# A few small numbers in one tile: every large tile starts 32 or 128 bytes earlier

## The chip, the core and the metric

The kernel runs on one core of a Trainium2 chip. The metric is the device time of one execution in microseconds. Three runs of the kernel before took 2431.29 to 2432.54 us, with a median of 2431.8 us.

Five engines work in parallel, each on its own list of instructions: PE (TensorE: weight loads and matmuls), DVE (VectorE), ACT (ScalarE), POOL (GpSimd, here mainly an issuer of DMAs) and SP (which issues DMAs). They wait for each other through semaphores. Tiles live in a memory of 128 partitions; an address below is the byte at which a tile starts within each partition.

## The reference

One layer of a streaming encoder on 256 tokens of 2048 features: a SwiGLU block, a gated mixer of two recurrent branches, a cross attention to 256 memory tokens, a second SwiGLU block, and a final norm. All of it is float32.

```python
x = x + 0.5 * swiglu(rms_norm(x, ffn1_norm[l]), ffn1_w_up[l], ffn1_w_down[l])
h = rms_norm(x, mix_norm[l])
proj = h @ w_in[l]                       # columns split into the branches' inputs and gates
y_a = ...                                # HGRN2 recurrence, normed, times silu(g_a)
y_b = ...                                # conv, RG-LRU scan, times gelu(gate_b)
merged = g[:, :, 0, :] * (y_a @ w_branch_a[l]) + g[:, :, 1, :] * (y_b @ w_branch_b[l])
x = x + merged @ w_out[l]
x = x + cross_attention(rms_norm(x, xattn_norm[l]), rms_norm(mem, mem_norm[l]), ...)
x = x + 0.5 * swiglu(rms_norm(x, ffn2_norm[l]), ffn2_w_up[l], ffn2_w_down[l])
return rms_norm(x, final_norm)
```

Each SwiGLU has 5632 hidden columns, so the two blocks hold most of the arithmetic.

## The kernel before

**How a product is made.** A float32 operand is split into a high and a low part of a shorter type (`split`: ACT copies the high part `h`, DVE subtracts it to get the low part `l`), and a product is a sum of matmuls high by high, high by low, and low by high. Weights arrive by DMA as `raw` tiles of 128 x 2048 floats (8192 bytes per partition) and are split into tiles `h` and `l` of the same size; in the SwiGLU blocks differences of weights (`td`, split into `h` and `tl`) save products. Activations stand in tiles of 128 x 1024 (4096 bytes) as `xh`, `xl`, `hidop`, `ops` and others. Each matmul has two operands in that memory: the stationary one, 128 columns wide, which a weight load (PEld) brings into the array, and the moving one, mostly 512 columns wide, which streams through.

- In the SwiGLU blocks (`three`), and in the products `rows_product`, a slice of an activation tile is stationary and a slice of `h`, `l` or `tl` moves: rows such as `acc<-h,xh` name the moving operand first, and then the stationary one.
- In `product` (middle part of the layer) the slice of the weight tile is stationary and the activation moves: `acc<-ops,h`.
- At the start the memory tokens, in tiles `ms` of 8192 bytes, are stationary, and their weights move: `acc<-h,ms` and `acc<-l,ms`.
- Hidden activations are transposed by PE against a constant identity: `acc<-vt,ev`.

**Where tiles lie.** Pools are laid out one behind the other, and each tile is rounded up to 32 bytes: `const` (small constants and the residual stream `x`), `big` (9 tiles of 8192 bytes), `slots` (24 tiles of 4096 bytes), `small` (a few bytes each), and then, in one region used in turn, the pools of a stage. In a SwiGLU stage this region holds four further tiles of 8192 bytes, pool `more`, which join the nine of `big` in one ring of 13: a tile `raw`, `h`, `l`, `td`, `tl`, `ev` or `ms` gets whichever of the 13 is free. In the middle stage the region holds other, smaller tiles, and the weight tiles use the nine of `big` alone.

**What sets the order.** Every instruction is recorded first (`Flow.record`), then a planner (`Flow.arrange`) orders each engine's list and chooses a place in the ring for each tile by estimated costs, and `Flow.emit` issues them all from one line. So the profile has line L478 for everything, and one goes by the names of tiles.

**What the change touches.** Three small tiles: `eps` (one number per partition, a bias for square roots), `rmtok` (two numbers: the norm factors of the memory tokens) and `ssm` (their sums of squares, in `head_squares`).

Of the kernel before, what the change touches and what calls it, by code (L numbers as in the profile page):

```python
# [9 lines left out]
F32 = mybir.dt.float32  # L10
F32R = mybir.dt.float32r
ACT = mybir.ActivationFunctionType
ALU = mybir.AluOpType

P = 128
T = 256
D = 2048
# [22 lines left out]
PAD = 16  # L40
# [149 lines left out]
class Flow:  # L190
# [22 lines left out]
    def pool(self, name, bufs, scope=None, **kw):  # L213
        self.pools.append(Pool(self, name, bufs, scope, **kw))
        return self.pools[-1]
# [267 lines left out]
def block_kernel(tc: tile.TileContext, xT, xin, memT, mem, vec, gfin, bgate, lruw, wu1, wd1, win, wv,  # L483
                 wg, wab, wout, wq, wk, wvm, wo, wu2, wd2, out_):
    flow = Flow(tc)
    pe, dve, act, sp, gps = flow.queues
    pool = flow.pool

    const = pool("const", 1)
    flow.share("big", pool("big", 9), 9)  # L490

    def big(name, dt=F32R):
        return flow.shared("big", [P, 2048], dt, name)

    slots = pool("slots", 24)
    small = pool("small", 2)
# [36 lines left out]
    warm = bank("warm")  # L533
    for _ in range(16):
        pe.matmul(warm[:, :P], ones, ones, start=True, stop=True)
    eps = const.tile([P, 1], F32, name="eps")
    act.activation(eps, ones[:, :1], ACT.Copy, scale=EPS)
    xt = [const.tile([P, 4 * T], F32, name=f"x{q}") for q in range(4)]
    x = [xt[k // 4][:, (k % 4) * T:(k % 4 + 1) * T] for k in range(KT)]
# [540 lines left out]
            self.tiles.append(self.cur[:, i * 512:(i + 1) * 512])  # L1080
            return self.tiles[-1]

    ms1, rmtok = BigOperands(), const.tile([P, 2], F32, name="rmtok")

    def head_memory(kq):
        m = slot(name="mem")
# [4 lines left out]
                ms1.add(m[:, j:j + T], col("mem_norm", 4 * kq + j // T))  # L1091

    def head_squares():
        ss = small.tile([P, 2 + PAD], F32, name="ssm", tag="ssm", bufs=1)[:, :2]
        for t in range(2):
            m = big("memory", F32)
            sp.dma_start(m, mem[t])
            act.activation(m, m, ACT.Square, accum_out=ss[:, t:t + 1])
        act.activation(ss, ss, ACT.Sqrt, bias=eps, scale=1.0 / D)
        dve.reciprocal(out=rmtok, in_=ss)  # L1100

    head.update({kq: lambda kq=kq: head_memory(kq) for kq in range(4)})
    todo = [[] for _ in range(11)]
    for p in range(8):
        todo[p].append(lambda p=p: head_x(p))
        if p % 2:
            todo[p].append(lambda p=p: sums1[p // 2]())
    todo[3].append(head_squares)
    for c in range(4):
        todo[6 + c].append(lambda c=c: head_residual(c))  # L1110
# [594 lines left out]
```

## Time and profile before

| | us |
|---|---|
| median of three runs | 2431.8 |
| the profiled execution | 2431.7 |
| its span, first to last instruction | 2429.9 |
| PE busy with matmuls | 2419.3 |
| PE busy with weight loads (beside the matmuls) | 2005.8 |
| DVE busy | 2090.5 |
| ACT busy | 1442.8 |

The first SwiGLU block fills the span up to about 760 us, the mixer and the attention stand between 760 and 1720 us, and the second SwiGLU block runs from about 1720 us to the end. Matmuls are pipelined: the duration shown for one is longer than the step from its start to the start of the next, so the pace of PE is read from starts. The timeline merges neighbours on one engine that have the same operands; a row gives the start of the first, the time to the end of the last, and their count. The step of one matmul is then the start of the next row minus the start of this one, divided by the count.

### The profile page before, as it was taken

The page shows a single profiled execution, that of the slowest core. Times are in us where ns is not written, and L with a number is a line of the kernel's source. Part 1 is how long each engine was busy: PE and PEld are TensorE (multiplying, and loading weights), DVE is VectorE, ACT ScalarE, POOL GpSimd, SP SyncE. Part 2 cuts the span into 40 slices and gives each one's busy share as a digit, 9 for nine tenths or more (in the row PEclk, how much of TensorE's full clock was granted, in tenths as well). Part 3 has the DMA queues.
Part 4 walks back from the last instruction along what each step waited for, and adds up shares of the span by engine and source line. Part 5 has one row for each costly group of instructions (what it writes and reads, how often), then busy time and mean ns, then how long its engine had stood idle before and what let it go on. Part 6 is the DMA issues. An engine that isn't in the chain of part 4 may idle for free. (4 is left out here: it accounts for less than half of the span.)

```text
span 2429.9 us, 31006 instructions
## 1 busy us (share of the span) xinstructions
PE 2419.3 (100%) x12105; PEld 2005.8 (83%) x12105; DVE 2090.5 (86%) x2270; ACT 1442.8 (59%) x1432; POOL 88.6 (4%) x149
## 2 busy tenths in 40 slices
PE   9999999999999999999999999999999999999998
PEld 8888788888888888888888888888878788888887
DVE  7899999999996677888787878887789999999994
ACT  8765666666665544445853455555676666665563
POOL 0000000000000000000000000000000000000000
PEclk9999999999999999999999999999999999999999
DMA  9675877777774578798898898887798667667773
GB/s 364 242 274 180 260 259 255 249 258 248 254 256 177 182 290 325 268 349 330 328 339 329 327 372 337 331 312 260 291 372 299 255 247 264 257 258 259 260 273 113
DMA packets 101235, 674.37 MB, mean 278 GB/s; under 512 B 11232, under 2 KB 12000, under 8 KB 27232
## 3 DMA queue, kind: packets, MB, share of 16 engines
q1 hardware_dynamic: 79776, 523.40, 57.5%
q0 software_dynamic: 20592, 147.86, 18.9%
q8 instruction: 95, 1.56, 0.2%
q10 hardware_dynamic: 720, 1.13, 0.1%
q14 instruction: 52, 0.43, 0.0%
HBM read 581.12 MB, written 62.91 MB: 265 GB/s over the span
## 5 line engine op out<-in xcount | busy, mean ns | idle before, releaser
L478 DVE TENSOR_TENSOR l<-raw,h 128x2048 fp32r<-128x2048 f32 (+2 forms) x425 | 860.1, 2028 | 173.9 <-ACT h L478 80.3
L478 ACT ACTIVATE h<-raw 128x2048 fp32r<-128x2048 f32 (+2 forms) x425 | 722.1, 1705 | 383.5 <-PE acc L478 176.2
L478 PE MATMUL acc<-h,xh 128*128 128x512 f32 x1237 | 476.8, 393 | 0.5 <-DVE ev L478 0.3
L478 PE MATMUL acc<-h,xl 128*128 128x512 f32 x1237 | 475.5, 392 | 0.0
L478 ACT ACTIVATE h<-td 128x1024 fp32r<-128x1024 f32 (+1 forms) x262 | 322.9, 1241 | 227.9 <-DVE td L478 171.7
L478 DVE TENSOR_TENSOR tl<-td,h 128x1024 fp32r<-128x1024 f32 (+1 forms) x262 | 375.6, 1448 | 8.6 <-PE acc L478 5.2
L478 PE MATMUL acc<-h,hidop 128*128 128x512 f32 x1408 | 360.7, 394 | 0.0
L478 PE MATMUL acc<-h,ops 128*128 128x512 f32 x1408 | 336.9, 391 | 0.0
L478 PEld LDWEIGHTS acc<-h,hidop 128*128 128x128 f32 x1408 | 262.9, 188 | 58.8
L478 PEld LDWEIGHTS acc<-h,ops 128*128 128x128 f32 x1408 | 262.7, 188 | 54.0
L478 PE MATMUL acc<-ops,h 128*128 128x512 f32 x1152 | 282.1, 393 | 0.2 <-DVE ops L478 0.2
L478 PEld LDWEIGHTS acc<-h,xh 128*128 128x128 f32 x1237 | 232.0, 188 | 54.9 <-ACT h L478 1.6
L478 PEld LDWEIGHTS acc<-h,xl 128*128 128x128 f32 x1237 | 232.4, 188 | 51.6
L478 PEld LDWEIGHTS acc<-ops,h 128*128 128x128 f32 x1152 | 211.4, 188 | 42.4 <-DVE ops L478 0.6
L478 PE MATMUL acc<-l,hidop 128*128 128x512 f32 x704 | 195.7, 392 | 0.0
L478 PE MATMUL acc<-tl,xh 128*128 128x512 f32 x636 | 177.4, 395 | 0.6 <-DVE tl L478 0.6
L478 PE MATMUL acc<-l,ops 128*128 128x512 f32 x704 | 174.3, 389 | 0.0
L478 PE MATMUL acc<-l,xh 128*128 128x512 f32 x601 | 169.8, 393 | 0.0
L478 DVE TENSOR_TENSOR made<-made 128x512 f32<-128x512 f32 x224 | 152.2, 688 | 9.1 <-DMA made<-wu 5.7
L478 PEld LDWEIGHTS acc<-l,hidop 128*128 128x128 f32 x704 | 132.2, 188 | 29.8
L478 PEld LDWEIGHTS acc<-ops,l 128*128 128x128 f32 x1152 | 150.5, 191 | 6.4
L478 PEld LDWEIGHTS acc<-l,ops 128*128 128x128 f32 x704 | 132.1, 188 | 27.4
(172 smaller groups left out, 2135.3 us busy)
## 6 DMA issues: line engine op xcount, KB each, us to landing
raw<-wu SPq DMA_DIRECT2D x109, 1024.0 KB, 6.2
raw<-wd SPq DMA_DIRECT2D x72, 1024.0 KB, 6.6
made<-wu POOLq DMA_DIRECT2D x56, 1024.0 KB, 6.7
kept<-made POOLq DMA_DIRECT2D x56, 1024.0 KB, 6.9
td<-kept SPq DMA_DIRECT2D x56, 1024.0 KB, 7.2
raw<-wu SPq DMA_DIRECT2D x56, 768.0 KB, 5.8
raw<-win SPq DMA_DIRECT2D x40, 1024.0 KB, 4.9
raw<-wg SPq DMA_DIRECT2D x32, 1024.0 KB, 6.6
```

Of the source, the lines that this page charges most:

```text
L478: getattr(op.queue.real, method)(*map(real, args), **{k: real(v) for k, v in kw.items()})
```

## The change

`eps`, `rmtok` and `ssm` become slices of one tile `few` of 8 floats, which is 32 bytes.

```diff
-    eps = const.tile([P, 1], F32, name="eps")
+    few = const.tile([P, 8], F32, name="few")
+    eps, rmtok, ssm = few[:, :1], few[:, 1:3], few[:, 3:5]
     act.activation(eps, ones[:, :1], ACT.Copy, scale=EPS)
...
-    ms1, rmtok = BigOperands(), const.tile([P, 2], F32, name="rmtok")
+    ms1 = BigOperands()
...
     def head_squares():
-        ss = small.tile([P, 2 + PAD], F32, name="ssm", tag="ssm", bufs=1)[:, :2]
         for t in range(2):
             m = big("memory", F32)
             sp.dma_start(m, mem[t])
-            act.activation(m, m, ACT.Square, accum_out=ss[:, t:t + 1])
-        act.activation(ss, ss, ACT.Sqrt, bias=eps, scale=1.0 / D)
-        dve.reciprocal(out=rmtok, in_=ss)
+            act.activation(m, m, ACT.Square, accum_out=ssm[:, t:t + 1])
+        act.activation(ssm, ssm, ACT.Sqrt, bias=eps, scale=1.0 / D)
+        dve.reciprocal(out=rmtok, in_=ssm)
```

Every engine's list holds the same instructions in the same order, with the same waits; only names differ. DVE's list shows it around the reciprocal of the memory tokens, some 70 rows from its start:

```order
 L478 TENSOR_TENSOR l<-raw,h 128x2048
 L478 RECIPROCAL rtok<-stdt 128x2
-L478 RECIPROCAL rmtok<-ssm 128x2
+L478 RECIPROCAL few<-few 128x2
 L478 TENSOR_TENSOR xl<-xg,xh 128x512
```

The instruction stands at the same place and handles the same two numbers. Each tile also keeps its place in its ring. What moves is the addresses, as the two built programs have them (start of the first tile; tiles follow at steps of their size):

| pool | tiles | start before | modulo 64 | start after | modulo 64 |
|---|---|---|---|---|---|
| `const`: `vt` with the identity, `ones` | 2 | 1152, 2784 | 0 and 32 | 1152, 2784 | 0 and 32 |
| `const`: `x` | 4 of 4096 | 3328 | 0 | 3328 | 0 |
| `const`: `rmtok` | 1 of 32 | 19712 | 0 | gone | |
| `big` | 9 of 8192 | 20128 | 32 | 20096 | 0 |
| `slots` | 24 of 4096 | 93856 | 32 | 93824 | 0 |
| `more` (SwiGLU stages) | 4 of 8192 | 192768 | 0 | 192640 | 0 |
| temporary tiles of the middle stage | 8 of 1024 and others | 192768 | 0 | 192640 | 0 |

The identity, a slice of `vt`, starts at 1824, which is 32 modulo 64, in both. `big` and `slots` move by 32 bytes, since `rmtok` no longer stands ahead of them; `more` and the temporary tiles move by 128 bytes, since the 96 bytes of `ssm` in `small` are gone too. Slices of these tiles that matmuls of 512 columns use begin at multiples of 512 bytes within the tile, so a slice has its tile's remainder.

## The prediction

> **What bounds the kernel now.** I read the page first, for the busy times and the chain that ended last, then the waits of PE.
>
> ```profile
> PE 2419.3 (100%) x12105; PEld 2005.8 (83%) x12105; DVE 2090.5 (86%) x2270; ACT 1442.8 (59%) x1432; POOL 88.6 (4%) x149
> ```
>
> ```profile
> engine line waited for: us in total, times, longest us
> PE warm L478 <- DVE ones L478: 1.1, 1, 1.1
> PE acc L478 <- DVE tl L478: 0.6, 3, 0.2
> ...
> ```
>
> PE is busy for 2419.3 of a span of 2429.9 us, and its waits are of 1 us and less each. So the time is the sum of the steps of 12,105 matmuls, and the change matters if it alters those steps. A busy PE need not be at its peak, so I read the steps from the timeline, in the order of time. In the middle of the layer, where all weight tiles lie in `big` and all activations in `slots`, a long run of matmuls with 512 columns reads:
>
> ```profile
> 1242.96 3.79 PE L478 MATMUL acc<-h,ops 128*128 128x512 f32 x16
> 1246.59 1.98 PE L478 MATMUL acc<-l,ops 128*128 128x512 f32 x8
> 1248.40 3.79 PE L478 MATMUL acc<-h,ops 128*128 128x512 f32 x16
> ```
>
> 24 matmuls from 1242.96 to 1248.40 us are 5.44 us, or 226.7 ns each. I call this the quiet step. The first stage is a test that this kernel makes by itself, because there moving and stationary tiles come from `big` and from `more` in every combination:
>
> ```profile
> 32.88 2.04 PE L478 MATMUL acc<-l,ms 128*128 128x512 f32 x8
> 34.75 3.82 PE L478 MATMUL acc<-h,ms 128*128 128x512 f32 x16
> 38.41 1.98 PE L478 MATMUL acc<-l,ms 128*128 128x512 f32 x8
> 40.23 3.84 PE L478 MATMUL acc<-h,ms 128*128 128x512 f32 x16
> 43.90 2.03 PE L478 MATMUL acc<-l,ms 128*128 128x512 f32 x8
> 45.77 3.89 PE L478 MATMUL acc<-h,ms 128*128 128x512 f32 x16
> 49.50 2.01 PE L478 MATMUL acc<-l,ms 128*128 128x512 f32 x8
> 51.35 3.79 PE L478 MATMUL acc<-h,ms 128*128 128x512 f32 x16
> 54.98 2.04 PE L478 MATMUL acc<-l,ms 128*128 128x512 f32 x8
> 56.85 0.86 PE L478 MATMUL acc<-h,ms 128*128 128x512 f32 x3
> ```
>
> With the tiles that the built program gives to these rows, and the remainders of their addresses modulo 64, the steps are:
>
> | row | moving | stationary | step, ns |
> |---|---|---|---|
> | 32.88, x8 | `more`, 0 | `big`, 32 | 233.8 |
> | 34.75, x16 | `big`, 32 | `big`, 32 | 228.8 |
> | 38.41, x8 | `big`, 32 | `big`, 32 | 227.5 |
> | 40.23, x16 | `more`, 0 | `more`, 0 | 229.4 |
> | 43.90, x8 | `big`, 32 | `more`, 0 | 233.8 |
> | 45.77, x16 | `more`, 0 | `big`, 32 | 233.1 |
> | 49.50, x8 | `big`, 32 | `big`, 32 | 231.3 |
> | 51.35, x16 | `big`, 32 | `big`, 32 | 226.9 |
> | 54.98, x8 | `more`, 0 | `big`, 32 | 233.8 |
>
> Where the remainders differ, a matmul takes 233 to 234 ns, whichever operand is the one at 0. Where they agree, at 32 or at 0, it takes 227, and the first dozen after a change of kind are still disturbed. That the pair 0 and 0 settles as well shows in its second half, asked for by itself:
>
> ```profile
> 42.08 1.98 PE L478 MATMUL acc<-h,ms 128*128 128x512 f32 x8
> 43.90 2.03 PE L478 MATMUL acc<-l,ms 128*128 128x512 f32 x8
> ```
>
> 1.82 us for 8 are 227.5 ns. After the change all large tiles stand at 0 modulo 64, so no such pair is unlike any more.
>
> **The change part by part.** *The small tiles.* The instructions that use `eps`, `rmtok` and `ssm` are the same in number, order and waits, so they cost nothing more; the last numbers are needed once, early.
>
> *DVE and ACT.* Their large operands move from 32 to 0 as well. Rows of one shape, whose tiles lie partly in `big` and partly in `more`, bound what that can do (minimum, median, maximum in ns):
>
> ```profile
> L478 DVE TENSOR_TENSOR td<-raw,td x206: 679/685/695, 78.5 to 2344.2; 128x512 f32<-128x512 f32 x103
> L478 DVE TENSOR_TENSOR td<-raw x103: 1215/1219/1227, 76.8 to 2339.7; 128x1024 f32<-128x1024 f32 x103
> ```
>
> The whole spread is 2% of the first and 1% of the second, with both remainders inside it. I take nothing, with 1% of DVE's time either way at the most, and DVE is not what PE waits for.
>
> *Unlike pairs.* By the built program's addresses, 1,978 of the matmuls with 512 columns have operands of unlike remainder: 1,858 in the two SwiGLU blocks, which is what 4 tiles of 13 would give, and 120 on the memory tokens. Each loses 233.75 - 226.7 = 7.05 ns: **13.9 us**.
>
> *The disturbed ones behind them.* In 284 places an unlike pair is followed by like ones. Row 34.75 gives 16 x (228.75 - 226.7) = 33 ns for one such place, row 49.50 gives 36. 284 x 33 ns are 9.4 us; some of these runs end before they have settled, so I take **8.1 us**.
>
> *The check from above.* The two SwiGLU blocks as a whole, first all instructions, and then those with the identity (the transposes); columns: the stretch, its length, busy us and count of PE, PEld, DVE, ACT and, where it worked, POOL, then the granted clock, the DMA engines' busy share and GB/s:
>
> ```profile
> 75.00:760.00 685.00, 684.42 (x3019) 557.78 (x3018) 639.03 (x656) 453.55 (x375) 25.07 (x30) 1.00 0.75 246
> 1720.00:2390.00 670.00, 669.51 (x2955) 544.27 (x2954) 630.72 (x539) 421.26 (x334) 0.00 (x0) 1.00 0.74 276
> ```
>
> ```profile
> 75.00:760.00 685.00, 12.61 (x96) 11.13 (x96) 2.21 (x8) 1.77 (x5) 1.00 0.75 246
> 1720.00:2390.00 670.00, 14.17 (x104) 12.15 (x104) 0.00 (x0) 3.20 (x8) 1.00 0.74 276
> ```
>
> ```profile
> 418.61 0.86 PE L478 MATMUL acc<-l,hidop 128*128 128x512 f32 x3
> 419.31 3.42 PE L478 MATMUL acc<-h,hidop 128*128 128x512 f32 x14
> 422.57 1.10 PE L478 MATMUL acc<-l,hidop 128*128 128x512 f32 x4
> ...
> 424.90 1.04 PE L478 MATMUL acc<-vt,ev 128*128 128x128 f32 x8
> 425.70 0.48 PE L478 MATMUL acc<-h,hidop 128*128 128x512 f32 x1
> ```
>
> Eight transposes take 425.70 - 424.90 = 0.80 us, or 100 ns each. At the quiet step the first block would need 2,923 x 226.7 ns + 96 x 100 ns = 672.2 us of its 685, the second 2,851 x 226.7 + 104 x 100 = 656.7 of 670: 12.8 and 13.3 us too much. These 26.1 us hold 13.1 of unlike pairs and 8 of disturbed ones, and leave 5 for what stays: PE's waits and the start after each group of transposes. The sum of 22.0 us fits under that bound.
>
> *New unlike pairs.* The identity stays at 32 modulo 64, and the tiles `ev`, `merge` and `p` that are transposed against it go to 0: 160 transposes become unlike. Group 424.90 is unlike already (its `ev` lies in `more`). Here is one with `ev` in `big`, alike:
>
> ```profile
> 300.07 1.03 PE L478 MATMUL acc<-vt,ev 128*128 128x128 f32 x8
> 300.86 1.40 PE L478 MATMUL acc<-h,hidop 128*128 128x512 f32 x5
> ```
>
> 0.79 against 0.80 us: nothing to pay. At most it is 160 x 7 ns, or 1.1 us.
>
> *What of it arrives.* A faster PE is of use only while its operands are there. The chain that ended last tells where they are not:
>
> ```profile
> 1901.25 1.68 DVE l L478
> ...
> 1918.07 2.30 DVE tl L478
> 1920.42 501.60 PE acc L478 x2210
> ```
>
> ```profile
> 0.00:60.00 60.00, 58.59 (x262) 48.09 (x263) 44.92 (x79) 49.24 (x89) 0.20 (x4) 1.00 0.96 366
> 1750.00:1950.00 200.00, 199.51 (x875) 160.07 (x874) 190.75 (x160) 135.15 (x103) 0.00 (x0) 1.00 0.81 306
> ```
>
> Up to 1920 us it runs over DVE, which is busy for 190.75 of 200 us there: PE takes `l` and `tl` as they are made. From 1920 us on it is PE alone. So the gain between 1750 and 1918 us can be lost: 22.0 us over the 1,355 us of the two blocks are 16 ns per us, times 168 us, 2.7 us. In the first 60 us the DMA engines are 96% busy and PE is fed by them: 0.9 us at most (80 unlike pairs and their followers). PE's waits for `tl` (0.6 us in all) mean that around them DVE sets the pace: I allow 1.6 us for the 100 us ahead of them. Of these 5.2 us I take two thirds, 3.5, since DVE itself waits for tiles that PE gives back, and gets these earlier. Behind that, what would be late next is DVE: its share rises from 93% and 94% of the two blocks (639.03 of 685, 630.72 of 670) to 95% and 96%, and PE stays the bound.
>
> The sum: 22.0 - 3.5 = **18.5 us** less. The profiled execution took 2431.7 us, 1.8 more than its span and 0.1 less than the median; 2431.8 - 18.5 = **2413.3 us**.
>
> *A rule that speaks against this.* The Trainium skill (TensorE: Matmul & The Clock Gate, "Step-by-step: what each phase is for") says that PE reads its moving and its stationary operand through two independent read ports, and prices a streamed matmul by its columns alone. By that rule addresses are free and the sum is 0. The rows of 32.88 to 56.85 us disagree with it by 7 ns per matmul, and the measurement decides.
>
> **The rivals.** *The region, not the remainder* (no change, 2431.8 us). In the kernel before, every tile at 0 also lies in the upper region, and what costs 7 ns could be that the operands lie far apart. Against it stands row 419.31: its moving tile is the first of `more` at 192768, and its first stationary tile lies at 179872, only 13 KB below, yet 14 matmuls take 3.26 us, 232.9 ns each. In rows 410.98 to 412.79 of the same timeline the moving tile is the first of `big`, at 20128, 160 KB from the same activations:
>
> ```profile
> 410.98 1.98 PE L478 MATMUL acc<-h,hidop 128*128 128x512 f32 x8
> 412.79 1.07 PE L478 MATMUL acc<-l,hidop 128*128 128x512 f32 x4
> ```
>
> 1.81 us for 8 are 226.3 ns. A border would have to fall just between the pools. The skill's rule of two ports would give the same 2431.8 us. Together 6%.
>
> *The pair 0 and 0 is worse than it looks* (slower). Only 40 matmuls of that kind exist before; afterwards all of some 9,570 with 512 columns are. All is lost from 226.7 + 22.0 us / 9,570 = 229.0 ns each on. Row 40.23 averages 229.4, and the other row with both tiles in `more` is worse:
>
> ```profile
> 66.07 2.01 PE L478 MATMUL acc<-l,ms 128*128 128x512 f32 x8
> 67.92 3.89 PE L478 MATMUL acc<-h,ms 128*128 128x512 f32 x16
> ```
>
> 1.85 us for 8 are 231.3 ns. If that were its lasting price, the time would be 9,570 x 2.3 ns = 22 us longer, 2454. Against it: this row follows unlike pairs as 49.50 does, which shows the same 231.3 ns with both at 32, and the settled half of row 40.23 is at 227.5. 4%.
>
> *DVE holds PE back* (faster by half). If the whole gain of the second SwiGLU block, about half of 22 us, were lost to DVE, since 94% busy leaves little room for jitter, the time would be 2431.8 - 11 + 1 = 2422. Against it: from 1920 us on, PE runs for 501.6 us without a link to another engine. 12%. If the first block lost its gain too, the change would not be measurable, 2%.
>
> **How the numbers follow.** My forecast has 76%: 2413.3 us. All of the gain, with the starts behind the transposes put right too, would be 24 us, so 2408; 13.9 us of unlike pairs with half of the followers, less all the 5.2 us, would be 12 to 13 us, so 2420. I take 2408 to 2420 as the range. A change of 0.2%, or 5 us, is about what a measurement here tells from none: faster by more has 88%, within it 8%, slower 4%.
>
> **What would show it.** In the profile after, rows with 512 columns should show steps of 226 to 228 ns throughout the SwiGLU blocks, whatever tile moves; the mean durations of groups such as `acc<-h,hidop` should fall to that of the quiet rows; the durations on DVE and ACT should stay. Waits of PE for `tl` and `h` near 270 and 1900 us should grow by 1 to 4 us in all. The prediction is wrong if unlike steps of 231 to 238 ns remain, if a lasting step at 0 and 0 lies above 229 ns, or if PE's waits swallow more than 6 us.

## The result, and the profile after

The changed kernel takes 2414.56 us (median of six runs, 2413.16 to 2415.67), beside 2431.84 us for the kernel before (six runs, 2431.29 to 2432.54). The ratio is 0.9928, with a 95% interval of 0.9916 to 0.9941: 17.3 us less. The profiled execution took 2415.09 us, and its span fell from 2429.9 to 2413.3 us, by 16.6.

The page's busy times after, and its waits of PE (us in total, times, longest):

```profile
PE 2401.9 (100%) x12105; PEld 2005.3 (83%) x12105; DVE 2088.1 (87%) x2270; ACT 1441.9 (60%) x1432; POOL 88.3 (4%) x149
```

```profile
engine line waited for: us in total, times, longest us
PE warm L478 <- DVE ones L478: 1.1, 1, 1.1
PE acc L478 <- DVE tl L478: 0.7, 3, 0.3
PE acc L478 <- DVE x L478: 0.5, 1, 0.5
PE acc L478 <- DVE l L478: 0.4, 1, 0.4
...
```

PE lost 17.4 us of busy time with the same 12,105 matmuls, while DVE, ACT and the weight loads stayed within 2.4 us. PE's waits stay below 1.2 us each; two are new, for `x` and for `l`. So it is the matmuls that became shorter. The timeline of PE in the first stage, where the rows before showed steps of 226.9 to 233.8 ns (start, time to the last end, matmuls):

```profile
33.26 1.98 PE L478 MATMUL acc<-l,ms 128*128 128x512 f32 x8
35.08 3.79 PE L478 MATMUL acc<-h,ms 128*128 128x512 f32 x16
38.70 1.98 PE L478 MATMUL acc<-l,ms 128*128 128x512 f32 x8
40.52 3.79 PE L478 MATMUL acc<-h,ms 128*128 128x512 f32 x16
44.14 1.98 PE L478 MATMUL acc<-l,ms 128*128 128x512 f32 x8
45.96 3.79 PE L478 MATMUL acc<-h,ms 128*128 128x512 f32 x16
49.58 1.98 PE L478 MATMUL acc<-l,ms 128*128 128x512 f32 x8
51.40 3.79 PE L478 MATMUL acc<-h,ms 128*128 128x512 f32 x16
55.02 1.98 PE L478 MATMUL acc<-l,ms 128*128 128x512 f32 x8
56.84 1.52 PE L478 MATMUL acc<-h,ms 128*128 128x512 f32 x6
```

Every row of 8 takes 1.82 us to the next start, every row of 16 takes 3.62 us: 226.3 to 227.5 ns per matmul, whichever tiles meet. The tiles and their order are those of the ten rows before.

The chain that ended last, from where PE takes over for good (before: 1920.42, 501.60 us):

```profile
1908.75 2.30 DVE tl L478
1911.05 0.04 issue
1911.10 494.30 PE acc L478 x2210
```

The same 2,210 matmuls take 7.3 us less, and PE starts them 9.3 us earlier: the gain comes from both SwiGLU blocks.

Both programs issue the same matmuls in the same order, so they can be matched one by one. The difference of their steps, from start to start, summed by kind (an unlike pair is one whose remainders modulo 64 differed before; a follower stands at most 16 matmuls behind one; waits are steps above 262 ns, other is everything that isn't a matmul of 512 columns, and the quiet rest, which changes by less than 0.1 us, has no column; + is gained):

| stretch of the kernel before, us | unlike pairs | followers | waits | other | in all |
|---|---|---|---|---|---|
| 0 to 60 | 0.3 | 0.1 | 0.7 | -1.2 | 0.0 |
| 60 to 400 | 3.1 | 1.4 | -0.4 | -0.3 | 3.7 |
| 400 to 450 | 0.6 | 0.1 | -1.6 | 0.0 | -0.8 |
| 450 to 760 | 3.1 | 1.7 | -0.2 | 0.0 | 4.5 |
| 760 to 1750 | 0.4 | 0.1 | 0.0 | 0.1 | 0.5 |
| 1750 to 1920 | 1.4 | 0.9 | -0.8 | -0.1 | 1.4 |
| 1920 to the end | 4.7 | 2.8 | -0.2 | 0.0 | 7.3 |
| sum | 13.5 | 7.1 | -2.5 | -1.4 | 16.6 |

The -1.2 us at the start are the warm-up matmuls, which took longer in this execution; they cost nothing, because PE would have waited for `ms` otherwise (11.09 us against 11.00 us for the same matmul). The one stretch where the change lost time, 400 to 450 us, is looked at further below.

### The profile page after: what moved, and what is told of

It reads as the page before. It is cut to its first block, busy times and chain, and to the rows that moved or that the text cites. A ratio compares the mean times of both kernels' runs of the same rounds, so it can differ in the third digit from the quotient of the medians.

```text
span 2413.3 us, 31006 instructions
## 1 busy us (share of the span) xinstructions
PE 2401.9 (100%) x12105; PEld 2005.3 (83%) x12105; DVE 2088.1 (87%) x2270; ACT 1441.9 (60%) x1432; POOL 88.3 (4%) x149
## 5 line engine op out<-in xcount | busy, mean ns | idle before, releaser
L478 PE MATMUL acc<-h,hidop 128*128 128x512 f32 x1408 | 355.8, 390 | 0.0
```

The lines of the kernel that those rows point to most:

```text
L478: getattr(op.queue.real, method)(*map(real, args), **{k: real(v) for k, v in kw.items()})
```

## The experiments

The theory going in: a matmul's step depends on where its moving and its stationary tile begin, one against the other. Open was whether the border (32 bytes, 64, more) is right, whether it is the pair that counts or an operand by itself, and whether anything else in the change helps. In all these kernels the instructions and their order are those after the change, and only addresses move. In the three kernels that move `more` alone, a few semaphore waits of SP and POOL differ as well; the one with 256 bytes has the same ones and keeps the whole gain, so it is not they that cost. A "gap" is an unused tile, opened ahead of a pool to push it up:

```diff
+GAP = {'more': 32}                # bytes ahead of a pool
...
                 if p.scope == scope:
+                    if p.name in GAP:
+                        g = stack.enter_context(tc.tile_pool(name=f"gap_{p.name}", bufs=1, **kw))
+                        gaps.append(g.tile([P, GAP[p.name] // 4], F32, name=f"gap_{p.name}{len(gaps)}"))
                     p.at = stack.enter_context(tc.tile_pool(name=p.name, bufs=1, **p.kw, **kw))
```

A "distance" below is the start of the moving slice minus that of the stationary one.

### `more` alone moved by 32 bytes

```diff
+GAP = {'more': 32}
```

> The changed kernel, with 32 unused bytes ahead of the four tiles of `more`, so that `more` alone goes back to 32 modulo 64 against 0 for all other large tiles. The three small tiles stay shared. Theory of the pair (a matmul loses 7 ns when its two operands start at unlike remainders modulo 64): the same 1,978 pairs are unlike as before the change, so all of the gain goes: 2431 to 2433 us, with steps of 231 to 238 ns where `more` moves. Rival, the small tiles (the shared tile itself or the smaller pool brought the gain): it stays at 2413 to 2416 us.

Measured: 2431.01 us (2430.09 to 2434.98), ratio to before 0.9999 (0.9990 to 1.0008). The whole gain is gone, although the small tiles are still one tile, `big` and `slots` still stand at 0 modulo 64, and the rest is as after the change. Matched with the kernel after, the pairs of `more` with another pool cost 12.4 us and their followers 6.9. So the relative position of `more` carries the gain.

### All large tiles at 32 modulo 64

```diff
+GAP = {'big': 32}
```

> The changed kernel, with 32 unused bytes ahead of `big`, so that `big`, `slots` and `more` all start at 32 modulo 64. Theory of the pair: no pair of 512 columns is unlike, so 2413 to 2416 us, as after the change. Rival, the boundary (a large tile that starts off a 64-byte boundary costs time by itself): all tiles are off it, slower than before the change; with 7 ns for each of 9,571 matmuls some 67 us more, about 2480 us.

Measured: 2414.62 us, ratio 0.9929 (0.9914 to 0.9944), which is the kernel after. That tiles begin at a multiple of 64 bytes is worth nothing; that they begin alike is worth the whole gain. It isn't the other address by itself that counts, it is that operands begin alike.

### `more` alone moved by 64 bytes

```diff
+GAP = {'more': 64}
```

> The changed kernel, with 64 unused bytes ahead of `more`: the operands of 1,978 matmuls differ by 64 modulo 128, and agree modulo 64. Theory of the pair with modulus 64: 2413 to 2416 us. Rival, modulus 128 (in the kernel before, the remainders modulo 128 were 0 and 32, so it does not tell the two apart): 2431 to 2433 us.

Measured: 2426.05 us, ratio 0.9977 (0.9968 to 0.9986). This fits neither: with a border of 64 all pairs would be alike and the time 2414.5, and 11.5 us of the gain are missing; with a border of 128 the time would be 2431 to 2433. The timeline of PE shows two kinds of step for one distance of 64 (a moving slice of `more`, a stationary one of `slots`):

```profile
419.05 3.37 PE L484 MATMUL acc<-h,hidop 128*128 128x512 f32 x14
422.25 1.08 PE L484 MATMUL acc<-l,hidop 128*128 128x512 f32 x4
...
543.08 3.20 PE L484 MATMUL acc<-h,hidop 128*128 128x512 f32 x13
546.11 1.10 PE L484 MATMUL acc<-l,hidop 128*128 128x512 f32 x4
```

14 matmuls take 3.20 us, 228.6 ns each, and 13 take 3.03 us, 233.1 ns each. In the first group single steps go round 226, 229 and 232 ns, in the second 233 and 234; of the 35 groups of 12 or more at 64, 32 go the first way. So "alike modulo 64" is too weak a rule, and 64 is a case between. What puts a group on one level or on the other isn't settled.

### `slots` alone moved by 32 bytes

`slots` moves by 32 bytes and `more` by 128, so that nearly every matmul with 512 columns is unlike, in the middle of the layer as well.

```diff
+GAP = {'slots': 32, 'small': 96}
```

> The changed kernel, with 32 unused bytes ahead of `slots` and 96 behind them: activations at 32, all weight tiles at 0 modulo 64, in the SwiGLU blocks and in the middle of the layer. 9,123 matmuls of 512 columns become unlike; only those on memory tokens and 64 others stay alike. Theory of the pair, a price per matmul: 9,123 x 7.05 ns = 64 us more than after the change, 2479 us; and up to 8 us more, 2487 us, if the 1,152 unlike matmuls of 256 columns pay as well. Rival, the region (only `more` against the rest costs): 2413 to 2416 us.

Measured: 2462.87 us, ratio 1.0127 (1.0110 to 1.0144), 48.3 us above the kernel after. The middle, where nothing was unlike before, in PE's timeline:

```profile
1257.81 3.90 PE L484 MATMUL acc<-h,ops 128*128 128x512 f32 x16
1261.54 2.03 PE L484 MATMUL acc<-l,ops 128*128 128x512 f32 x8
1263.41 3.90 PE L484 MATMUL acc<-h,ops 128*128 128x512 f32 x16
```

3.73 us for 16 and 1.87 for 8 are 233.1 and 233.8 ns: the unlike step, now far from `more` and its region. The sum came out lower than expected. Matched with the kernel after, 9,116 matmuls at a distance other than 0 modulo 256 (among them some 120 between `more` and `big`, which stand at 128 here) cost 55.7 us, 6.1 ns each and not 7; the waits of PE fell by 4.1 us, since a slower PE is kept waiting less; and the 1,152 matmuls with 256 columns that became unlike were faster, by 3.0 us in all. That last part was not foreseen, and the last experiment takes it up.

### A map of distances

Each of the nine tiles of `big` begins at another offset within its place, and the places are 256 bytes longer, so that one kernel holds many distances.

```diff
+GAP = {'slots': 256}
+SKEW = (0, 16, 32, 48, 64, 96, 128, 192, 256)
...
-                    x.at = p.at.tile(x.shape, x.dt, name=x.name, tag=f"{x.ring.tag}{i}")
+                    n = x.shape[1]
+                    wide = [P, n + 64] if p.name == "big" else x.shape
+                    x.at = p.at.tile(wide, x.dt, name=x.name, tag=f"{x.ring.tag}{i}")
+                    if p.name == "big":
+                        x.at = x.at[:, SKEW[i] // 4:SKEW[i] // 4 + n]
```

> The changed kernel, with each of the nine tiles of `big` at another distance from the activations: modulo 512 the nine weight tiles start 0, 272, 32, 304, 64, 352, 128, 448 and 256 bytes behind the remainder of `slots` and `more`. One look, for the steps of single tiles in the middle of the layer, and not for the total. The theory of the pair with modulus 64 is hurt by the run with 64 bytes, which lost 11.5 of the 17 us. Theory of the bare distance: only a distance of 0 (modulo 512) runs at 226.7 ns, and all others cost 2 to 7 ns, 128 and 256 too. Rival, modulus 128: 128 and 256 run at 226.7 ns like 0, 64, 352 and 448 at 229 to 234, the rest at 231 to 238. Rival, modulus 256: only 256 does.

Measured: 2448.28 us in a single run. The time itself says little, the steps say it all. Two pieces of PE's timeline, with the distances modulo 512 from the built program: 128, 272 and 64 for the first three rows, then 0, 448, 256 and 352:

```profile
1273.64 3.89 PE L489 MATMUL acc<-h,ops 128*128 128x512 f32 x16
1277.37 2.02 PE L489 MATMUL acc<-l,ops 128*128 128x512 f32 x8
1279.22 3.82 PE L489 MATMUL acc<-h,ops 128*128 128x512 f32 x16
1282.88 0.39 PE L489 MATMUL acc<-l,ops 128*128 128x512 f32 x1
...
1382.92 3.83 PE L489 MATMUL acc<-h,ops 128*128 128x512 f32 x16
1386.58 2.03 PE L489 MATMUL acc<-l,ops 128*128 128x512 f32 x8
1388.45 3.81 PE L489 MATMUL acc<-h,ops 128*128 128x512 f32 x16
1392.09 2.04 PE L489 MATMUL acc<-l,ops 128*128 128x512 f32 x8
1393.98 1.03 PE L489 MATMUL acc<-vt,x 128*128 128x128 f32 x8
```

From start to start: 233.1 ns at 128, 231.3 at 272, 228.8 at 64; 228.8 at 0, 233.8 at 448, 227.5 at 256, and 236 at 352, with the disturbed ones at the head of each row in the mean. With only those matmuls that have at least eight of the same distance ahead of them, the whole trace gives:

| distance modulo 512 | settled step, ns | matmuls |
|---|---|---|
| 0 | 227.0 | 775 |
| 256 | 227.2 | 126 |
| 64 | 229.2 | 157 |
| 320 | 228.5 | 8 |
| 32, 48, 128, 160, 208, 240, 272, 304, 352, 384, 448, 480 | 231.6 to 234.0 | the rest |

Only 0 and 256 are quiet. 128, which is alike modulo 64 and modulo 128, takes 233.1 ns. So among the distances tried, which are multiples of 16 bytes, the border is 256. On the way to it 64 (and 320, which is 64 modulo 256) costs less than the others; 448, which is 64 in the other direction, doesn't.

### The identity alike as well

`few` doubled and another 8 numbers in the tile of constants bring the identity and `ones` to 0 modulo 64, where the transposed tiles are. By the border of 256 only the transposes of `x` become alike (distance 0); those of `ev`, `merge` and `p` go from 160 to 128.

```diff
-    ("conv_b", 8), ("ba", 8), ("bx", 8),
+    ("conv_b", 8), ("ba", 8), ("bx", 8), ("gap", 8),
...
-    few = const.tile([P, 8], F32, name="few")
+    few = const.tile([P, 16], F32, name="few")
```

> The changed kernel, with 32 unused bytes ahead of the identity in `vt` and a shared tile of 64 bytes, so that the identity and the constant ones too start at 0 modulo 64, like all large tiles. Tests the term 'new unlike pairs', which was put at nothing with a bound of 1.1 us. If it is nothing: 2414 to 2415.5 us, and 0.79 us for a group of eight transposes, as before. If unlike transposes pay 7 ns each, and the starts behind them as well, 1 to 3.5 us less than after the change: 2411 to 2413.5 us.

Measured: 2415.23 us (2414.24 to 2416.42), ratio 0.9933 (0.9920 to 0.9947): no difference from the kernel after. Eight transposes, in PE's timeline of the kernel after and then of this one:

```profile
421.58 1.04 PE L478 MATMUL acc<-vt,ev 128*128 128x128 f32 x8
422.37 2.07 PE L478 MATMUL acc<-h,hidop 128*128 128x512 f32 x8
```

```profile
421.51 1.04 PE L478 MATMUL acc<-vt,ev 128*128 128x128 f32 x8
422.30 1.86 PE L478 MATMUL acc<-h,hidop 128*128 128x512 f32 x7
```

0.79 us in both. Transposes of `x` step by 108.9 ns here at distance 0, and by 109.0 ns after the change at 32. Over the runs above, steps between transposes average 108.8 to 109.2 ns at 0, 32, 96, 128 and 160 modulo 256. For these transposes the distance costs nothing.

### `more` alone moved by 256 bytes

```diff
+GAP = {'more': 256}
```

> 256 unused bytes ahead of the four tiles of `more`, so that they lie 256 bytes further from `big` and `slots` than after the change, with all distances still 0 modulo 256. Theory (a matmul is quiet where moving and stationary tile start a multiple of 256 bytes apart): 2414.5 us, within 2 us. Rival (what counts is a larger modulus, 512 or 1024, and the single tile at 256 in the map run settled for another reason): the 1,978 pairs of `more` with another pool become slow again, 2427 to 2431 us.

Measured: 2415.01 us (2414.84 to 2415.94), ratio 0.9931 (0.9915 to 0.9947): the kernel after again. Of the four moves of `more` alone (0, 32, 64 and 256 bytes), 0 and 256 have the whole gain, 64 has a third of it, and 32 has none. The border of 256 bytes holds for the time of the whole kernel.

### Only the matmuls with 256 columns unlike

The low weight tiles of the products with moving activations (`l`, here called `lc`) begin 64 bytes into their place; the 9,571 matmuls with 512 columns keep distances of 0 modulo 256.

```diff
+SKEW = 64
+GAP = {'slots': 256}
...
+                    wide = [P, n + 64] if p.name == "big" else x.shape
...
+                        x.at = x.at[:, (SKEW // 4 if x.name == "lc" else 0):][:, :n]
...
```

> The low weight tiles of the middle stage alone (`l` of the products with activations moving, called `lc` here) start 64 bytes into their place; all other distances stay 0 modulo 256. So only the 1,152 matmuls with 256 columns, `acc<-ops,lc`, are unlike. Theory A (an unlike matmul of 256 columns is faster, 116.5 to 117.6 ns in the map run against 119.1 to 119.4, and nothing follows it): 1,152 x 1.5 to 2.9 ns are 1.7 to 3.3 us less than after the change, 2411.3 to 2412.9 us. Theory B (as fast, but the matmuls of 512 columns behind each of the 72 groups of 16 are disturbed by about 30 ns, as behind other unlike matmuls): 2 us come back, 2413.4 to 2415 us. Theory C (no gain at all for 256 columns by themselves; what was seen came from their neighbours being unlike too): 2414.6 to 2417 us.

Measured: 2413.08 us (2411.85 to 2415.45), ratio to before 0.9925 (0.9911 to 0.9939). A period of one product, 16 matmuls with 256 columns and 16 with 512, in PE's timeline after the change and then here:

```profile
793.52 2.08 PE L478 MATMUL acc<-ops,l 128*128 128x256 f32 x16
795.43 3.82 PE L478 MATMUL acc<-ops,h 128*128 128x512 f32 x16
799.09 2.08 PE L478 MATMUL acc<-ops,l 128*128 128x256 f32 x16
```

```profile
797.36 2.05 PE L489 MATMUL acc<-ops,lc 128*128 128x256 f32 x16
799.25 3.81 PE L489 MATMUL acc<-ops,h 128*128 128x512 f32 x16
802.90 2.05 PE L489 MATMUL acc<-ops,lc 128*128 128x256 f32 x16
```

1.91 us for 16 became 1.89, and the 16 behind them take 3.66 and 3.65 us. Over all, the step with 256 columns falls from 119.4 to 117.8 ns, which is 1.9 us, and the matmuls of 512 columns behind them change by less than 0.1 us. So theory A holds by the steps: with 256 columns unlike is better, and nothing follows it. The time of the kernel doesn't decide: 2413.08 lies between what A gave (2412.9 at most) and what B gave (2413.4 at least), and 1.5 us between two medians whose runs overlap is too little to be called measured.

## Why the prediction was right, and where its steps were not

**The mechanism was right, and its rule was too weak.** The profile before could show that unlike pairs cost 7 ns, and the runs confirm that it is the pair: all at 32 is as good as all at 0, and one pool moved takes everything back. But the prediction read the border as 64 bytes. Before the change the pairs of `more` with another pool lay at a distance of 96 modulo 256 (1,922 of them) or, with the roles exchanged, of 160 (56), and all others at 0, since their tiles and pools lie multiples of 256 apart. So the trace held a distance of 0 and of 96 either way, and could not tell 64 from 256. That the changed addresses are alike modulo 256 too (192640 - 20096 = 674 x 256) was not asked; in this point the forecast was lucky. With `more` 64 bytes further on, the same argument would have given 2413 where 2426 was measured.

**Unlike pairs, 13.9 us.** Measured 13.5, or 6.8 ns each for 1,978. The term held.

**Disturbed followers, 8.1 us.** Measured 7.1, 25 ns per place and not 28.5. The price of 33 ns came from a row in which 16 matmuls follow and settle. The 114 places with at least 12 followers did cost 32 ns each, but 170 of the 284 end before that and cost 20: the discount for them was too small. The term was mis-sized by 1 us.

**The check from above, 26.1 us** held as a bound: the two terms as measured come to 20.6 us, below it.

**New unlike transposes, 0.** Right: 0.79 us for eight as before, and the same with the identity moved.

**DVE and ACT, nothing.** Right. The groups of DVE whose tiles lie in both pools, after:

```profile
L478 DVE TENSOR_TENSOR td<-raw,td 128x512 f32<-128x512 f32 x206 | 140.6, 683 | 0.7
...
L478 DVE TENSOR_TENSOR td<-raw 128x1024 f32<-128x1024 f32 x103 | 125.3, 1217 | 3.5 <-DMA raw<-wu 2.7 <-PE acc L478 0.7
```

Their means are 683 and 1217 ns; the means before were 686 and 1220.

**What doesn't arrive, 3.5 us.** In all 4.0 us of the 20.6 didn't arrive (13.5 + 7.1 - 16.6). The size was near, the places were not. Between 1750 and 1918 us, where 2.7 us were held to be at risk, 0.8 were lost although the chain of waits runs over DVE there; near 250 to 300 us 0.2, of 1.6 allowed. In the first 60 us, where 0.9 were held to be at risk, the 0.4 us gained were lost; by the built program's addresses 48 unlike pairs run there, and the prediction's 80 are reached at 72 us. The largest loss, 1.6 us, lies at 400 to 450 us, which the prediction didn't name. PE's timeline there after the change, then DVE's:

```profile
415.46 3.33 PE L478 MATMUL acc<-h,hidop 128*128 128x512 f32 x14
419.17 1.20 PE L478 MATMUL acc<-l,hidop 128*128 128x512 f32 x4 [0.38 <-DVE l L478]
...
430.40 0.39 PE L478 MATMUL acc<-h,xl 128*128 128x512 f32 x1
431.31 0.50 PE L478 MATMUL acc<-h,xh 128*128 128x512 f32 x1 [0.52 <-DVE x L478]
```

```profile
416.83 2.28 DVE L478 TENSOR_TENSOR l<-raw,h 128x2048 fp32r<-128x2048 f32 x1
```

And the same tile on DVE before:

```profile
419.55 2.28 DVE L478 TENSOR_TENSOR l<-raw,h 128x2048 fp32r<-128x2048 f32 x1
```

Before, `l` was finished at 421.83 us and PE began to use it at 422.57 (a row that the prediction shows): 0.74 us to spare. After, it is finished at 419.11 us, 2.7 us earlier, but PE is through with the 14 matmuls ahead by about 418.6 us, 3.9 us earlier, and waits. This place lost 0.63 us. The wait for `x` behind it lost a little more, 0.77 us, in the same way. DVE's row after, and then before:

```profile
430.57 0.68 DVE L478 SCALAR_TENSOR_TENSOR x<-acc,x 128x512 f32<-128x512 f32 x1
```

```profile
432.78 0.68 DVE L478 SCALAR_TENSOR_TENSOR x<-acc,x 128x512 f32<-128x512 f32 x1
```

Before, this `x` was finished at 433.46 us, and the same matmul started at 434.00: 0.54 us to spare. After, `x` is finished 2.2 us earlier, and PE could have started 3.4 us earlier. So the slack was in the trace before, for `l` at a row that the prediction used for something else. It wasn't read because the prediction looked for danger where PE already waited, and a wait that is about to appear has no row among the waits. The loss varies: the same stretch lost 2.2 us with all tiles at 32, 0.7 with the identity moved, and 0.3 with the low tiles moved.

**The rivals.** *The region* falls with the first two experiments: in the kernel with `more` moved by 32 bytes the regions are those of after, and the time is that of before. *The pair 0 and 0* falls with the steps of 226 to 227.5 ns. *DVE holds PE back* falls by the last stretch of the table: 7.3 us arrive behind 1920 us, of 7.5 gained there. *Addresses are free*, the rival that the prediction drew from a rule, falls too: the starts of the two operands, one against the other, move the step by 6 to 7 ns in 227. The rule is in the Trainium skill (TensorE: Matmul & The Clock Gate, "Step-by-step: what each phase is for"): throughput goes by the columns alone, and the two operands have independent read ports. For the time of a matmul with 512 columns this kernel's traces don't agree with the first half, by those 6 to 7 ns; whether the ports are independent no run here shows.

**The sum.** 22.0 - 3.5 was 18.5; measured 20.6 - 4.0 is 16.6 in the profiled execution, and 17.3 between the medians. The difference from the forecast of 2413.3 us is the followers (1.0), the unlike pairs (0.4) and what didn't arrive (0.5), with 0.7 back from the profiled execution to the median.

## What to carry to other kernels

Where PE is the bound and the step of equal matmuls varies, sort the steps by the distance between the starts of the moving and the stationary slice: here 0 modulo 256 gave 227 ns with 512 columns, and nearly every other distance 231 to 234. It costs at most 255 bytes per pool and partition to lay pools out at multiples of 256 bytes of one another, and a few bytes of small tiles between them are enough to spoil it. A rule read from two cases should be tried at the values that the trace doesn't hold before it is called a rule; and where the bound engine gets faster, the next waits stand where its operands are ready with less to spare than it gains, not only where it waits already.

## What the runs showed of the hardware that was not expected

- The step of a matmul with 512 columns depends on the distance of its operands modulo 256, not 64: 227 ns at 0, 229 at 64 in the settled mean of the map, 231.6 to 234 elsewhere. At 64 bytes groups settle at one of two levels, 228.6 or 233.1 ns. Why the distance matters at all, why 64 stands out, and what chooses the level stays open.
- With 256 columns the sign is the other way: 119.4 ns alike, 117.8 at a distance of -64 bytes, and 116.9 with `slots` moved by 32. The runs don't show why.
- Transposes with the identity don't feel the distance: 108.8 to 109.2 ns from one to the next at 0, 32, 96, 128 and 160 modulo 256.
- When the distance changes, the next dozen matmuls are uneven even if they are alike (nearly all single steps between 224 and 240 ns), and cost about 25 ns together. A kernel with mixed distances pays for each change of kind as well: a third of the gain here, 7.1 of 20.6 us.
